# Two layers and a second block on one core: products over 64 rows of the array widened to all 128

## The chip, the cores and the metric

The kernel runs on one core of a Trainium2 chip. The metric is the device time of one execution in microseconds (us), and less is better. TensorE is called PE here (its weight loads PEld), VectorE DVE, ScalarE ACT, GpSimd POOL, SyncE SP.

## What is computed

512 tokens of 2048 features pass through two equal layers and then a second block. Each layer multiplies x by a wide matrix, feeds three branches (a short convolution, a causal attention with eight heads, a linear recurrence called rwkv), mixes them with a second matrix and normalises. The second block has a differential attention with eight heads and a state space branch. Three places matter here. In the rwkv branch of both layers:

```python
r, wd, k, v, ad = _split(xs, RWKV_SHIFT_SIZES)          # wd, ad: 64 features each
w = -jax.nn.softplus(-(w0 + jnp.tanh(wd) @ w2)) - 0.5   # w2: 64 x 512
a = jax.nn.sigmoid(a0 + ad @ a2)                        # a2: 64 x 512
```

In the attention of both layers the scores of a head are a product over 192 features, 128 of its own and 64 rotary ones whose key all heads share:

```python
q = jnp.concatenate([q_nope, _rope(q_pe, cos, sin)], axis=-1)
k = jnp.concatenate([k_nope, jnp.broadcast_to(k_pe, (B, S, MLA_HEADS, QK_ROPE))], axis=-1)
s = jnp.einsum('bqhd,bkhd->bhqk', qb, k, preferred_element_type=jnp.float32) * scale
```

In the second block each head has two score maps, each a product over 64 features:

```python
s = jnp.einsum('bqhcd,bkhcd->bhcqk', q_blk, k).astype(jnp.float32) * scale
p = jax.nn.softmax(s, axis=-1)
w = p[:, :, 0] - lam * p[:, :, 1]
```

## The kernel before

Everything lies with features on the 128 partitions and the 512 tokens in the free dimension. Nearly all the work of PE is the wide products of `inproj` (L184 to L186): a weight is split into a high and a low part (ACT casts the high one at L169, DVE subtracts for the low one at L170), x is split in the same way, and of the four products three are made, tile by tile of 128 features. A tile of 128 output columns takes 16 tiles of features times three products, each 128 rows by 512 tokens.

Products over 64 features are handled in a more compact way. One operand holds its high part on one half of the partitions and its low part on the other half, the second operand holds its high part on both halves, so that one product over 128 rows gives high times high and low times high. What is missing, high times low, is a second product over the 64 partitions of the own half. There are three such places:

- `rank_product` (L481): L484 over 128 rows, L485 over 64 rows, 512 tokens each. It is called twice by `rwkv_prep` for each of four pairs of heads, in two layers: 16 times. `rwkv_lora` (L463 to L478) makes its operands; one tile `wl` holds the low parts of both weights, on a half each.
- `scores` in `mla_branch` (L921): for each of four query tiles L929 over 128 rows, L930 over 64 rows, then L931 over 128 rows in plain float32; eight heads, two layers: 64 times.
- `diff_scores` (L1585): for each of four query tiles and two components L1632 over 128 rows, L1633 over 64 rows; eight heads: 64 times. Component 0 lies on partitions 0 to 63, component 1 on 64 to 127, and one tile `kl` holds the low parts of the keys of both.

The query tiles have 256, 256, 384 and 512 columns.

No order is written by hand. The framework orders the instructions of each engine from its own estimate of durations, and each engine then runs its list strictly in order. Tiles come from pools with a fixed number of slots; a tile whose slot is still in use waits. In the second block the attention's pool `qa` has 20 slots under the tag `a`, handed out in turn. Constants (masks, the rotary tables `cos` and `sin`) live in the pool `cp` for the whole kernel.

In each layer the masked products of a chunk (L560) give DVE and POOL the blocks to be inverted in `rwkv_inverse` (L598, L599); PE meanwhile works on other columns, and the first instruction of PE that needs the inverse's space is L664 in `rwkv_chunks`, which reads what was spilled to DRAM under the name `pack`. POOL's sums of squares (L774) and small powers (L397) of the low rank projections stand in POOL's list ahead of its share of the inverse.

Of the kernel before, what the change touches and what calls it, by code (L numbers as in the profile page):

```python
# [19 lines left out]
P = 128  # L20
S = 512
# [34 lines left out]
# column starts in w_in  # L56
# [3 lines left out]
# rows of the packed layer parameters  # L60
# [13 lines left out]
class K:  # L74
    """What every part of the kernel shares: engines, pools, constants."""
# [23 lines left out]
    def open(self, name, psum, side=None, **bufs):  # L99
        """pools for one part of the kernel: slots of 2 KB, and of 4 KB where the tag ends in 4; psum: its banks.  # L100
        To be closed; tags of the parts around it stay in use."""
# [43 lines left out]
    def load_w(self, parts, kt, n, side=False):  # L145
        """parts: [(source [kt*P, m], first column of the tile)]; for each k the two exact parts, or one tile of
        them side by side."""
# [26 lines left out]
    def split(self, src, hi, lo, eng=None):  # L174
        """hi + lo == src, each in eleven bits of mantissa."""
        self.nc.scalar.copy(hi, src)
        return (eng or self.nc.vector).tensor_tensor(out=lo, in0=src, in1=hi.bitcast(F32), op=ALU.subtract)  # L177

    def mm3(self, out, w, x, first=True, last=True):
        """out[m, n] (+)= sum over k of w[k][., m] x[k][., n] in three passes; w, x: lists of (hi, lo)."""  # L180
# [13 lines left out]
    def inproj_group(self, x, cols, pss):  # L194
        """several tiles of columns at once, tile by tile of x as they come"""
# [11 lines left out]
def bc_last(ap, n):  # L207
    """[p, a] seen as [p, a, n]"""
    return ap.unsqueeze(2).to_broadcast([ap.shape[0], ap.shape[1], n])


def consts(k: K):
# [5 lines left out]
    # blk[p, q] = 1 where p and q lie in the same block of 64, blk32 of 32  # L218
# [9 lines left out]
    # [s, (strict t > s, incl t >= s)] in each block of 64  # L228
    k.mrk = cp.tile([P, P], F32, name="mrk")
# [6 lines left out]
    # scan resets: zero at the start of each 64  # L236
    k.rst = cp.tile([P, S], F32, name="rst")
    nc.gpsimd.memset(k.rst, 1.0)
    nc.gpsimd.memset(k.rst.rearrange("p (c t) -> p c t", t=64)[:, :, 0:1], 0.0)
    # causal: 0 where key <= query, NEG elsewhere, [q, k]  # L240
# [4 lines left out]
    # dup[p, m]: the sum of the two halves of the rows, onto both  # L245
    k.dup = cp.tile([P, P], F32, name="dup")
# [9 lines left out]
def rope_tables(k: K, positions):  # L256
    nc, cp = k.nc, k.cp
    k.cos = cp.tile([P, S], F32, name="cos")
    k.sin = cp.tile([P, S], F32, name="sin")
# [21 lines left out]
    # with the sign of the product that goes to the other half of each 64  # L281
# [4 lines left out]
def _reduce_angle(self, ang):  # L286
    """ang less its nearest multiple of two pi"""
# [15 lines left out]
def layer_params(k: K, a, l):  # L303
    """The per-feature vectors of a layer, one column each; in two steps."""
# [45 lines left out]
    # 1 - mu, half of w0 and a0, 1 - k_a  # L350
# [10 lines left out]
def tok_sums(k: K, tiles, rhs, ncol, width=None):  # L361
    """[128 tokens, 4, ncol] of sum over features of tile * rhs column; tiles: list of [P, S]"""
# [8 lines left out]
def bcast_cols(k: K, cols, nh):  # L371
    """PSUM [P, S] whose row p, column t is cols[t % 128, t // 128, head of p]; cols: SBUF [P, 4, nh]"""
# [13 lines left out]
def rsqrt_cols(k: K, ps, shape, scale, eps, floor=None):  # L386
    """(scale * ps + eps) ** -0.5, or max(ps, floor) ** -0.5"""
# [13 lines left out]
def gate2(k: K, ps, out=False):  # L401
    """2 * silu of a PSUM tile; out: let go of the tile soon"""
# [11 lines left out]
def shifted(k: K, ps, mu, omu, tag=None):  # L414
    """token shift of a projection: (1 - mu) u + mu * (u one token earlier)"""
# [33 lines left out]
def rwkv_first(k: K, x, w):  # L449
    """the products for the ranks of the decay and the rate and for the first pair of heads"""  # L450
# [7 lines left out]
def rwkv_lora(k: K, a, l, ps, col, der):  # L458
# [4 lines left out]
    # for products in two passes: of the decay's and the rate's ranks the high part on their own half of the partitions  # L463
    # and the low one on the other, the weights' high part on both and the low one on the own
    hs, out, wl = (slice(0, 64), slice(64, 128)), [], k.b(dt=F32R)
    for q, key in enumerate(("rwkv_w2", "rwkv_a2")):
# [5 lines left out]
        wh, r = k.b(dt=F32R), k.b(dt=F32R)  # L472
        nc.scalar.copy(wh, w2)
        nc.vector.tensor_tensor(out=wl[own], in0=w2[own], in1=wh.bitcast(F32)[own], op=ALU.subtract)
        nc.scalar.copy(r[own], wa[own])
        nc.vector.tensor_tensor(out=r[other], in0=wa[own], in1=r.bitcast(F32)[own], op=ALU.subtract)
        out.append((wh, r, wl, own))
# [3 lines left out]
def rank_product(k: K, ranks, c):  # L481
    (wh, r, wl, own), cols = ranks, slice(c, c + P)
    ps = k.ps()
    k.nc.tensor.matmul(ps, lhsT=wh[:, cols], rhs=r, start=True, stop=False)  # L484
    k.nc.tensor.matmul(ps, lhsT=wl[own, cols], rhs=r[own], start=False, stop=True)  # L485
# [3 lines left out]
# a pair of heads' operands for 128 tokens, in floats of a row: [B|K] of the first chunk of 64 and [K|B] of the  # L489
# second; V, its chunks swapped; A; R; for each head and chunk the masked products [B|K] x [A|R], [s, (A|R, t)]  # L490
# [12 lines left out]
def rwkv_prep(k: K, l, j, rkv, col, der, ranks, pe, T, pack, sbg):  # L503
# [3 lines left out]
    # decay: log w = -(c/2)(1 + tanh(z/2)), its sums over each chunk  # L507
# [13 lines left out]
    # in-context rate  # L521
# [4 lines left out]
    # kk = normalised k * k_k  # L526
# [6 lines left out]
    # A = -kk * Pex ; B = kk * a / P ; K = k' / P ; R = r * P  # L533
# [20 lines left out]
    # products of the tokens of a chunk  # L554
# [16 lines left out]
    # bonus: (sum over a head of r k' r_k) v  # L571
# [7 lines left out]
def rwkv_inverse(k: K, T, TI):  # L579
    """inverses of the 64 x 64 blocks on the diagonal of 1 - T, row by row of T; of each block one partition has  # L580
    the even rows and another the odd ones"""
# [12 lines left out]
    def step(eng, X, tmp, q, n, w):  # L594
        """the first n rows of X, whose last w columns come after T's row q"""
# [30 lines left out]
def rwkv_chunks(k: K, pe, pack, TI, Y):  # L626
    """the states and outputs of all heads, 128 tokens of two pairs at a time"""
# [938 lines left out]
def ssm_glu(k: K, a, yp, src, sz):  # L1566
# [15 lines left out]
    return out  # L1582


def diff_scores(k: K, hd, x, w, first):  # L1585
    nc = k.nc
    V, G = nc.vector, nc.gpsimd
    hm = k.hm
# [211 lines left out]
```

## Time and profile before

| | |
|---|---|
| three runs | 3482.21, 3482.34, 3485.09 us; median 3482.34 us |
| profiled execution, first to last instruction | 3480.9 us |
| PE busy | 97% of the span, 15603 matmul records |
| DVE, ACT, POOL busy | 58%, 34%, 25% |
| mean granted clock of PE | 0.980 of full speed |
| HBM traffic | 364.93 MB read, 92.27 MB written |

A matmul's busy time in this profile is longer than its share of the engine, because matmuls overlap: L184 has a mean of 398 ns although one starts every 0.23 us. So what a matmul costs is read from the distance of starts in the timeline, not from its duration. The time of the profiled execution itself is not listed apart from the three runs; its span is 1.4 us below their median.

### The profile page before, as it was taken

The page shows a single profiled execution, that of the slowest core. Times are in us where ns is not written, and L with a number is a line of the kernel's source. Part 1 is how long each engine was busy: PE and PEld are TensorE (multiplying, and loading weights), DVE is VectorE, ACT ScalarE, POOL GpSimd, SP SyncE. Part 2 cuts the span into 40 slices and gives each one's busy share as a digit, 9 for nine tenths or more (in the row PEclk, how much of TensorE's full clock was granted, in tenths as well). Part 3 has the DMA queues.
Part 4 walks back from the last instruction along what each step waited for, and adds up shares of the span by engine and source line. Part 5 has one row for each costly group of instructions (what it writes and reads, how often), then busy time and mean ns, then how long its engine had stood idle before and what let it go on. Part 6 is the DMA issues. An engine that isn't in the chain of part 4 may idle for free.

```text
span 3480.9 us, 41882 instructions
## 1 busy us (share of the span) xinstructions
PE 3360.1 (97%) x15603; PEld 2666.2 (77%) x15603; DVE 2003.3 (58%) x3035; ACT 1194.4 (34%) x1950; POOL 861.0 (25%) x974
## 2 busy tenths in 40 slices
PE   8999899999999998999988999999999999999999
PEld 7777688777867776887767666777777888888887
DVE  4546645655754466355589688878787532332332
ACT  4332223543533322224457233333333422222332
POOL 1224322003411143230035233333333000000011
PEclk9999999999989999999999899999999999999999
DMA  6455445335644454443256343433433733333443
GB/s 174 146 171 151 128 126 154 104 101 146 209 135 134 148 148 134 121 153 116 76 183 221 99 131 106 121 112 116 119 115 94 228 106 108 105 100 106 151 141 117
DMA packets 687934, 466.27 MB, mean 134 GB/s; under 512 B 91285, under 2 KB 621994, under 8 KB 687730
## 3 DMA queue, kind: packets, MB, share of 16 engines
q1 hardware_dynamic: 687730, 463.59, 44.9%
q8 instruction: 123, 2.02, 0.3%
q14 instruction: 81, 0.66, 0.1%
HBM read 364.93 MB, written 92.27 MB: 131 GB/s over the span
## 4 chain that ended last, share of the span: by engine, by line
PE 40%; DVE 9%; issue 3%; DMA 1%; ACT 1%; POOL 0%; SPq 0%; DVEq 0%; ACTq 0%
PE acc L186 10%; PE acc L185 10%; PE acc L184 10%; PE ps_b L186 2%; PE ps_b L185 2%; PE ps_b L184 2%; DVE wl L170 1%; DVE s L1537 1%; DVE x L1541 1%; PE ps_s L1552 1%; PE ps_s L931 1%; PE ps_a L1633 1%; DVE x L1542 1%; DVE b L1159 1%; DVE x L1538 1%
## 5 line engine op out<-in xcount | busy, mean ns | idle before, releaser
L186 PE MATMUL acc<-xh,wl 128*128 128x512 f32 x3552 | 1409.9, 397 | 19.4 <-DVE wl L170 19.4
L184 PE MATMUL acc<-xh,wh 128*128 128x512 f32 x3552 | 1406.7, 398 | 10.3 <-ACT u L1501 4.9
L185 PE MATMUL acc<-xl,wh 128*128 128x512 f32 x3552 | 1410.5, 397 | 2.2 <-DVE xl L177 2.2
L170 DVE TENSOR_TENSOR wl<-wr,wh 128x1024 fp32r<-128x1024 f32 (+1 forms) x508 | 676.3, 1332 | 820.1 <-ACT wh L169 807.4
L169 ACT CAST wh<-wr 128x1024 fp32r<-128x1024 f32 (+1 forms) x508 | 530.5, 1044 | 1529.7 <-PE acc L185 1208.4
L186 PEld LDWEIGHTS acc<-xh,wl 128*128 128x128 f32 x3552 | 674.6, 190 | 175.3 <-DVE wl L170 24.6
L184 PEld LDWEIGHTS acc<-xh,wh 128*128 128x128 f32 x3552 | 674.8, 190 | 167.5 <-issue 12.4
L185 PEld LDWEIGHTS acc<-xl,wh 128*128 128x128 f32 x3552 | 674.3, 190 | 164.3 <-issue 20.2
L1733 POOL TENSOR_TENSOR b<-b,b 128x512 f32<-128x512 f32 x16 | 20.9, 1309 | 496.1 <-DVE b L1731 496.1
L1532 POOL TENSOR_TENSOR s<-s,s 128x512 f32<-128x512 f32 x32 | 44.7, 1397 | 263.0 <-DVE s L1531 256.0
L1731 DVE SCALAR_TENSOR_TENSOR b<-b,ps_b 128x512 f32<-128x512 f32 x32 | 22.0, 688 | 106.0 <-PE ps_b L186 106.0
L1154 POOL TENSOR_TENSOR b<-b,b 128x512 f32<-128x512 f32 x28 | 46.7, 1667 | 112.1 <-DVE b L1137 97.4
L397 POOL TENSOR_TENSOR rr_a<-rv_a,mhalf 128x8 f32<-128x8 f32 (+1 forms) x24 | 46.6, 1940 | 108.8 <-DVE rv_a L392 108.8
L1552 PE MATMUL ps_s<-x,s 128*32 128x512 f32 x128 | 46.9, 672 | 27.4 <-DVE x L1541 27.4
L1540 POOL TENSOR_TENSOR s<-s,x 128x512 f32<-128x512 f32 x32 | 52.0, 1625 | 82.9 <-DVE x L1538 58.5
L1474 POOL TENSOR_TENSOR r<-r,r 128x512 f32<-128x512 f32 x32 | 55.8, 1744 | 63.3 <-DVE r L1473 57.5
L961 POOL TENSOR_TENSOR v<-v,c 128x512 f32<-128x512 f32 x16 | 20.6, 1286 | 204.6 <-ACT v L958 197.2
L598 DVE TENSOR_TENSOR pk<-pk,pk 128x224 f32<-128x224 f32 (+59 forms) x126 | 65.4, 519 | 4.5 <-DMA pk<-T 1.1
L599 DVE TENSOR_TENSOR pk<-pk,pk 128x224 f32<-128x224 f32 (+59 forms) x126 | 64.4, 511 | 3.5
L655 POOL COPY zm_pk<-pk 64x128 f32<-64x128 f32 x64 | 27.1, 424 | 151.3 <-DMA pk<-pack 138.0
L819 ACT ACTIVATE a<-ps_a,nm_a,sp_a 128x128 f32<-128x128 f32 (+3 forms) x64 | 39.2, 615 | 69.9 <-DVE nm_a L816 65.8
L563 DVE TENSOR_TENSOR pk<-ps_m,mrk 128x512 f32<-128x512 f32 x32 | 22.1, 691 | 68.3 <-PE ps_m L560 68.2
(497 smaller groups left out, 4486.0 us busy)
## 6 DMA issues: line engine op xcount, KB each, us to landing
wr<-in_w_in_dram SPq DMA_DIRECT2D x336, 512.0 KB
wr<-in_w_out_dram SPq DMA_DIRECT2D x96, 512.0 KB
pack<-pk SPq DMA_DIRECT2D x32, 576.0 KB
pk<-pack SPq DMA_DIRECT2D x32, 576.0 KB
CS<-r SPq DMA_DIRECT2D x32, 512.0 KB
s<-CS SPq DMA_DIRECT2D x32, 512.0 KB
b<-xd SPq DMA_DIRECT2D x48, 256.0 KB
c<-mix SPq DMA_DIRECT2D x32, 256.0 KB
```

The lines of the kernel that those rows point to most:

```text
L169: nc.scalar.copy(hi[:, : m * n], raw[:, : m * n])
L170: nc.vector.tensor_tensor(out=lo[:, : m * n], in0=raw[:, : m * n], in1=hi.bitcast(F32)[:, : m * n], op=ALU.subtract)
L184: self.nc.tensor.matmul(out, lhsT=wh, rhs=xh, start=st, stop=False)
L185: self.nc.tensor.matmul(out, lhsT=wh, rhs=xl, start=False, stop=False)
L186: self.nc.tensor.matmul(out, lhsT=wl, rhs=xh, start=False, stop=sp)
L397: nc.gpsimd.tensor_tensor(out=r.rearrange(flat), in0=v.rearrange(flat), in1=k.mhalf[:, 0:n], op=ALU.pow)
L598: eng.tensor_tensor(out=t3, in0=X[:, 0:n, c - 1 : c].to_broadcast([P, n, w]), in1=q[:, q.shape[1] - w :].unsqueeze(1).to_broadcast([P, n, ...
L599: eng.tensor_tensor(out=X[:, 0:n, c:], in0=X[:, 0:n, c:], in1=t3, op=A)
L1154: nc.gpsimd.tensor_tensor(out=sums[0], in0=sums[0], in1=t, op=ALU.add)
L1474: nc.gpsimd.tensor_tensor(out=x, in0=x, in1=m, op=SB)
L1540: G.tensor_tensor(out=t1, in0=sn, in1=t2, op=M)
L1552: nc.tensor.matmul(py[o], lhsT=lc[:, d, o], rhs=xs[p][d], start=(d == 0), stop=(d == 1))
```

## The change

The second product runs over all 128 rows in all three places. For the rank products each weight gets a low part on both halves (`wl` inside the loop, and six slots in the pool `wa` in place of five). For the attention of the layers the shared key's low part was already on both halves, so only the slices go. In the second block each component gets a low tile of its own, whose other half is zero; `diff_lows` makes two such pairs once and sets the zeros with four POOL instructions, and heads use the pairs in turn. With two halves multiplied, the rank products and the layers' scores now also contain low times low; in the second block the zeros leave the result as it was. Five constants of the two layers move to a pool `lp` that closes ahead of the second block, and `qa` has 19 slots under `a` in place of 20.

```diff
 def rwkv_lora(k: K, a, l, ps, col, der):
...
-    hs, out, wl = (slice(0, 64), slice(64, 128)), [], k.b(dt=F32R)
+    hs, out = (slice(0, 64), slice(64, 128)), []
...
-        wh, r = k.b(dt=F32R), k.b(dt=F32R)
+        wh, r, wl = k.b(dt=F32R), k.b(dt=F32R), k.b(dt=F32R)
         nc.scalar.copy(wh, w2)
-        nc.vector.tensor_tensor(out=wl[own], in0=w2[own], in1=wh.bitcast(F32)[own], op=ALU.subtract)
+        nc.vector.tensor_tensor(out=wl, in0=w2, in1=wh.bitcast(F32), op=ALU.subtract)
...
 def rank_product(k: K, ranks, c):
...
-    k.nc.tensor.matmul(ps, lhsT=wl[own, cols], rhs=r[own], start=False, stop=True)
+    k.nc.tensor.matmul(ps, lhsT=wl[:, cols], rhs=r, start=False, stop=True)
...
     def scores(hd, pair):
...
-            nc.tensor.matmul(ps[:, 0:m], lhsT=qp[h][hs, ts], rhs=kpl[hs, 0:m], start=False, stop=False)
+            nc.tensor.matmul(ps[:, 0:m], lhsT=qp[h][:, ts], rhs=kpl[:, 0:m], start=False, stop=False)
...
-        with k.phase(f"p{l}a", {"x": 3, "m": 1}, w=10, r=5, pk=2, wa=5):
+        with k.phase(f"p{l}a", {"x": 3, "m": 1}, w=10, r=5, pk=2, wa=6):
...
+def diff_lows(k: K):
+    out = []
+    for _ in range(2):
+        kl = [k.small((P, S), f"kl{c}", 2, F32R) for c in range(2)]
+        for c, t in enumerate(kl):
+            k.nc.gpsimd.memset(t[64 - 64 * c : 128 - 64 * c].bitcast(F32), 0.0)
+        out.append(kl)
+    return out
...
-def diff_scores(k: K, hd, x, w, first):
+def diff_scores(k: K, hd, x, w, first, kl):
...
-        qs, ks, kl = [k.b(dt=F32R) for _ in range(2)], [k.b(dt=F32R) for _ in range(2)], k.b(dt=F32R)
+        qs, ks = [k.b(dt=F32R) for _ in range(2)], [k.b(dt=F32R) for _ in range(2)]
...
-            V.tensor_tensor(out=kl[own], in0=kr[own], in1=ks[c].bitcast(F32)[own], op=ALU.subtract)
+            V.tensor_tensor(out=kl[c][own], in0=kr[own], in1=ks[c].bitcast(F32)[own], op=ALU.subtract)
...
-                nc.tensor.matmul(ps[:, 0:m], lhsT=qs[c][halves[c], i * P : n], rhs=kl[halves[c], 0:m], start=False, stop=True)
+                nc.tensor.matmul(ps[:, 0:m], lhsT=qs[c][:, i * P : n], rhs=kl[c][:, 0:m], start=False, stop=True)
...
-    att = k.open("qa", {"a": 3}, "right", a=20)
+    att = k.open("qa", {"a": 3}, "right", a=19)
...
+        with k.use("a", "a"):
+            lows = diff_lows(k)
...
-                nxt = diff_scores(k, q, x, w, first[1:] if q == 0 else [])
+                nxt = diff_scores(k, q, x, w, first[1:] if q == 0 else [], lows[q % 2])
...
 def fused_kernel(ctx: ExitStack, tc: tile.TileContext, a, out, dbg=None):
     k = K(ctx, tc, dbg)
+    layers = ExitStack()
+    k.lp = layers.enter_context(tc.tile_pool(name="lp", bufs=1))
...
         x, xd = first_layer(k, a, l, x, xd, *k.par[l])
+    layers.close()
     second_block(k, a, x, xd, out)
```

The tiles `mrk`, `rst`, `dup`, `cos` and `sin` take `k.lp` where they took `cp`.

The number of instructions stays the same on PE, DVE, ACT and SP; POOL has four more. The framework's order moves in places. Three are shown, in the names that the program gives its tiles; the line numbers of the changed kernel differ, since L1632 and L1633 became L1642 and L1643.

The first is PE in the second block, at the first head's scores (`ps_a` is the score tile, `acc` a wide product in progress). Before:

```order
L1632 MATMUL ps_a_16856<-a_16773,a_16771 128x256
L1633 MATMUL ps_a_16856<-a_16775,a_16771 128x256
L186 MATMUL acc_17068<-xh_16339,wl_17064 128x512
L184 MATMUL acc_17068<-xh_16348,wh_17063 128x512
L1632 MATMUL ps_a_16869<-a_16774,a_16772 128x256
L185 MATMUL acc_17068<-xl_16349,wh_17063 128x512
L1633 MATMUL ps_a_16869<-a_16775,a_16772 128x256
L186 MATMUL acc_17068<-xh_16348,wl_17064 128x512
```

With the change:

```order
L1642 MATMUL ps_a_16869<-a_16787,a_16785 128x256
L1643 MATMUL ps_a_16869<-kl_a_16412,a_16785 128x256
L186 MATMUL acc_17081<-xh_16344,wl_17077 128x512
L184 MATMUL acc_17081<-xh_16353,wh_17076 128x512
L1642 MATMUL ps_a_16882<-a_16788,a_16786 128x256
L185 MATMUL acc_17081<-xl_16354,wh_17076 128x512
L1643 MATMUL ps_a_16882<-kl_a_16413,a_16786 128x256
L186 MATMUL acc_17081<-xh_16353,wl_17077 128x512
```

Nothing moved here: the second product of a score tile has products over 128 rows on both sides in either list, and reads `kl_a` in the new one.

The second is PE in the first layer around L664, the first use of what the inverse leaves free. Before:

```order
L186 MATMUL acc_3928<-xh_139,wl_3918 128x512
L184 MATMUL acc_3928<-xh_150,wh_3917 128x512
L664 MATMUL ps_t_2749<-ident,pk_2740 128x128 x4
L185 MATMUL acc_3928<-xl_151,wh_3917 128x512
L186 MATMUL acc_3928<-xh_150,wl_3918 128x512
```

With the change:

```order
L185 MATMUL acc_3864<-xl_164,wh_3853 128x512
L186 MATMUL acc_3864<-xh_164,wl_3854 128x512
L184 MATMUL acc_3864<-xh_175,wh_3853 128x512
L664 MATMUL ps_t_2753<-ident,pk_2744 128x128 x4
L185 MATMUL acc_3864<-xl_176,wh_3853 128x512
```

L664 now stands one column tile earlier (`acc_3864` is the tile that was `acc_3860`, the one ahead of `acc_3928`): 42 wide products that preceded it now follow it, and 43 in the second layer. The last masked products L560 stand 32 wide products earlier too in the first layer, and 41 in the second.

The third is POOL in the first layer, ahead of its share of the inverse (`la` and `c`: sums of squares, `pk` and `t_pk`: the inverse). Before:

```order
L635 MEMSET zq_pk_2731 128x512
L397 TENSOR_TENSOR rr_c_2495<-rv_c_2493,mhalf 128x4
L608 MEMSET pk_2010 128x1024
L608 MEMSET pk_2011 128x512
L610 MEMSET pk_2010 64x16 x2
L610 MEMSET pk_2011 64x16 x2
L774 TENSOR_TENSOR la_2506<-la_2506,c_2636 128x512
L397 TENSOR_TENSOR rr_c_2648<-rv_c_2646,mhalf 128x4
L598 TENSOR_TENSOR t_pk_2012<-pk_2011,pk_2086 128x31
```

With the change:

```order
L774 TENSOR_TENSOR la_2221<-la_2221,c_2351 128x512
L608 MEMSET pk_2014 128x1024
L608 MEMSET pk_2015 128x512
L774 TENSOR_TENSOR la_2221<-la_2221,c_2419 128x512
L610 MEMSET pk_2014 64x16 x2
L610 MEMSET pk_2015 64x16 x2
L774 TENSOR_TENSOR la_2221<-la_2221,c_2487 128x512
L397 TENSOR_TENSOR rr_c_2499<-rv_c_2497,mhalf 128x4
L774 TENSOR_TENSOR la_2510<-la_2510,c_2640 128x512
L598 TENSOR_TENSOR t_pk_2016<-pk_2015,pk_2090 128x31
```

Three of the sums moved from ahead of the clearing instructions to among them, and the last L397 moved behind the first steps of the inverse.

## Rows read from the trace of the kernel before

**Rows 1.** The page: span, and part 1 for PE (busy us, share, instructions).
```profile
span 3480.9 us, 41882 instructions
...
PE 3360.1 (97%) x15603; PEld 2666.2 (77%) x15603; DVE 2003.3 (58%) x3035; ACT 1194.4 (34%) x1950; POOL 861.0 (25%) x974
```
**Rows 2.** Timeline of PE, rank products: start, us, line, out<-in, rows*columns, moving operand.
```profile
74.41 0.39 PE L484 MATMUL ps_x<-wa,wa 128*128 128x512 f32 x1
74.73 0.50 PE L485 MATMUL ps_x<-wa,wa 64*128 64x512 f32 x1
75.16 0.49 PE L484 MATMUL ps_x<-wa,wa 128*128 128x512 f32 x1
75.58 0.49 PE L485 MATMUL ps_x<-wa,wa 64*128 64x512 f32 x1
76.01 0.50 PE L184 MATMUL acc<-xh,wh 128*128 128x512 f32 x1
76.35 0.40 PE L185 MATMUL acc<-xl,wh 128*128 128x512 f32 x1
76.59 0.40 PE L186 MATMUL acc<-xh,wl 128*128 128x512 f32 x1
```
**Rows 3.** Timeline of PE in the second block: products over 96 rows.
```profile
2010.01 0.63 PE L1528 MATMUL ps_s<-us_s,s 96*128 96x512 f32 x2
2010.48 0.39 PE L186 MATMUL acc<-xh,wl 128*128 128x512 f32 x1
```
**Rows 4.** Timeline of PE's weight loads at the rank products.
```profile
74.19 0.19 PEld L484 LDWEIGHTS ps_x<-wa,wa 128*128 128x128 f32 x1
74.73 0.18 PEld L485 LDWEIGHTS ps_x<-wa,wa 64*128 64x128 f32 x1 [0.35 <-issue]
```
**Rows 5.** Stages of layer one: us; busy (count) PE, PEld, DVE, ACT, POOL; clock.
```profile
60.00:285.00 225.00, 223.41 (x1054) 176.28 (x1053) 102.03 (x121) 71.33 (x96) 62.51 (x96) 1.00 0.53 161
...
600.00:790.00 190.00, 188.81 (x851) 140.78 (x849) 111.63 (x246) 92.33 (x198) 19.14 (x20) 1.00 0.40 120
```
**Rows 6.** The same for one head of the second block, in two parts.
```profile
2304.00:2347.00 43.00, 43.00 (x182) 32.27 (x183) 25.67 (x61) 20.33 (x37) 2.38 (x3) 1.00 0.39 114
2347.00:2396.00 49.00, 45.13 (x205) 32.38 (x205) 48.36 (x56) 10.53 (x23) 31.30 (x19) 0.97 0.39 115
```
**Rows 7.** Timeline of PE in the second block: one score tile of 256 columns.
```profile
2140.50 0.28 PE L1632 MATMUL ps_a<-a,a 128*128 128x256 f32 x1
2140.71 0.38 PE L1633 MATMUL ps_a<-a,a 64*128 64x256 f32 x1
2141.02 0.50 PE L184 MATMUL acc<-xh,wh 128*128 128x512 f32 x1
2141.35 0.39 PE L185 MATMUL acc<-xl,wh 128*128 128x512 f32 x1
```
**Rows 8.** Timeline of PE in the layers' attention: products of 256 columns over 128 rows.
```profile
658.51 0.28 PE L915 MATMUL acc<-wh,n 128*128 128x256 f32 x1
...
658.86 0.28 PE L915 MATMUL acc<-wh,n 128*128 128x256 f32 x1
```
**Rows 9.** Timeline of PE in the layers' attention: a score tile.
```profile
641.15 0.28 PE L929 MATMUL ps_s<-n,q 128*128 128x256 f32 x1
641.36 0.38 PE L930 MATMUL ps_s<-n,q 64*128 64x256 f32 x1
641.67 0.49 PE L931 MATMUL ps_s<-q,q 128*128 128x128 f32 x2
```
**Rows 10.** Waits of PE, second block (1990 to 2700): total us, times, longest.
```profile
PE ps_s L1552 <- DVE x L1541: 27.4, 12, 4.0
```
**Rows 11.** Waits of PE during the first layer's inverse (285 to 376).
```profile
PE ps_t L664 <- DMA pk<-pack: 15.3, 1, 15.3
```
**Rows 12.** Timeline of POOL: its first step of that inverse.
```profile
318.55 1.30 POOL L598 TENSOR_TENSOR t_pk<-pk,pk 128x31 f32<-128x31 f32 x1 [2.91 <-DMA pk<-T]
```
**Rows 13.** Line L635: a POOL clearing instruction, ns min/median/max.
```profile
L635 POOL MEMSET zwh_pk<- x4: 518/523/529, 283.1 to 1250.7; 128x512 f32 x4
```

More of the change, by code (lines that the diff above doesn't have):

```diff
@@ L227, in consts @@
     k.hm = k.blk64.rearrange("p (h w) -> p h w", w=64)[:, :, 0]
-    k.mrk = cp.tile([P, P], F32, name="mrk")
+    k.mrk = k.lp.tile([P, P], F32, name="mrk")
     mk = k.b((P, 2, P))
@@ L235, in consts @@
         nc.gpsimd.tensor_copy(out=k.mrk[a : a + 64].rearrange("p (i t) -> p i t", i=2), in_=mk[a : a + 64, :, a : a + 64])
-    k.rst = cp.tile([P, S], F32, name="rst")
+    k.rst = k.lp.tile([P, S], F32, name="rst")
     nc.gpsimd.memset(k.rst, 1.0)
@@ L244, in consts @@
                             channel_multiplier=1)
-    k.dup = cp.tile([P, P], F32, name="dup")
+    k.dup = k.lp.tile([P, P], F32, name="dup")
     for half in (0, 64):
@@ L257, in rope_tables @@
     nc, cp = k.nc, k.cp
-    k.cos = cp.tile([P, S], F32, name="cos")
-    k.sin = cp.tile([P, S], F32, name="sin")
+    k.cos = k.lp.tile([P, S], F32, name="cos")
+    k.sin = k.lp.tile([P, S], F32, name="sin")
     row = k.b()
@@ L471, in rwkv_lora @@
             nc.sync.dma_start(out=w2[h], in_=a[key][l])
-        wh, r = k.b(dt=F32R), k.b(dt=F32R)
+        wh, r, wl = k.b(dt=F32R), k.b(dt=F32R), k.b(dt=F32R)
         nc.scalar.copy(wh, w2)
-        nc.vector.tensor_tensor(out=wl[own], in0=w2[own], in1=wh.bitcast(F32)[own], op=ALU.subtract)
+        nc.vector.tensor_tensor(out=wl, in0=w2, in1=wh.bitcast(F32), op=ALU.subtract)
         nc.scalar.copy(r[own], wa[own])
         nc.vector.tensor_tensor(out=r[other], in0=wa[own], in1=r.bitcast(F32)[own], op=ALU.subtract)
-        out.append((wh, r, wl, own))
+        out.append((wh, r, wl))
     return out
 def rank_product(k: K, ranks, c):
-    (wh, r, wl, own), cols = ranks, slice(c, c + P)
+    (wh, r, wl), cols = ranks, slice(c, c + P)
     ps = k.ps()
     k.nc.tensor.matmul(ps, lhsT=wh[:, cols], rhs=r, start=True, stop=False)
-    k.nc.tensor.matmul(ps, lhsT=wl[own, cols], rhs=r[own], start=False, stop=True)
+    k.nc.tensor.matmul(ps, lhsT=wl[:, cols], rhs=r, start=False, stop=True)
     return ps
@@ L923, in scores @@
         h = hd % 2
-        hs = slice(h * 64, h * 64 + 64)
         prs = []
```

## Prediction

> **What bounds the kernel now.** I read the page first: PE is busy for 97% of a span of 3480.9 us, DVE for 58% [rows 1]. Matmuls overlap in this profile, so 97% only says that PE is rarely without work, not that it works at its best pace. The next view is therefore the timeline of PE, where the distance between starts tells what each matmul really takes.
>
> At the rank products the reader sees the price of a change of width [rows 2]. Between two neighbours over 128 rows with 512 columns the distance is 0.24 us (76.35 to 76.59). From a product over 128 rows to one over 64 it is 0.32 (74.41 to 74.73), from the 64 rows back to 128 it is 0.43 and 0.43 (74.73 to 75.16, 75.58 to 76.01), and the neighbour after that is late too: 0.34 (76.01 to 76.35). A product over 96 rows pays nothing of this: two of them and the step to L186 take 0.47, which is 0.235 each [rows 3]. So it isn't a matter of rows left idle; something is paid at the border between 64 rows and more, in both directions. The weight loads show the same border: the load of L484 starts at 74.19, a whole matmul ahead of its product at 74.41, while that of L485 starts at 74.73, together with its own product [rows 2, 4].
>
> Then the stages. In the part of a layer with the rank products PE is busy for 223.41 of 225 us and DVE for 102.03; in the one with the attention scores PE has 188.81 of 190 and DVE 111.63 [rows 5]. The second layer repeats both. A head of the second block has two faces: while its scores are made PE is busy all 43 us and DVE 25.67, and in the state space part DVE is the full one with 48.36 of 49 us, PE having 45.13 [rows 6].
>
> **The change, part by part.**
>
> *Rank products, 16.* From L484 at 74.41 to L185 at 76.35 there are five steps in 1.94 us [rows 2]. At 0.235 each they would be 1.18. The two products over 64 rows therefore cost 0.76 together, 0.38 each. Widened, they have neighbours of the same kind on both sides and take the common pace. 16 x 0.38 = 6.1 us, all of it on the path, since PE is what fills that stage [rows 5].
>
> *Scores of the second block, 64.* From L1632 at 2140.50 to L185 at 2141.35 are 0.85 us for two products of 256 columns and one of 512 [rows 7]. The pace of 256 columns over 128 rows is a third of 658.51 to 658.86, 0.117 [rows 8]. Expected without a border: 2 x 0.117 + 0.235 = 0.47. The excess is again 0.38. 64 x 0.38 = 24.3 us. The wider tiles cross the same borders, so I use one number for all.
>
> *Scores of the layers' attention, 64.* The steps into and out of L930 are 0.21 and 0.31 [rows 9], equal to those of L1633 (2140.50 to 2140.71, 2140.71 to 2141.02) [rows 7], so the same 0.38 applies: 24.3 us, in a stage that PE fills [rows 5].
>
> Together 54.7 us of PE's time. The ends for the unknown price of the widened product: it cannot well save more, for that a step would have to be below the common pace, and no row shows one; it may save less, if only the two steps around the product go and the lateness of the one after them stays. Without that last step, which is 0.10 too long (2141.02 to 2141.35, less 0.235) [rows 7], it is 0.28 each, or 40 us. I take 0.38, since 96 rows pass with no lateness on either side [rows 3].
>
> *How much of it arrives.* The first 30.4 us lie in stages that PE fills, and I count them whole. In the second block the scores lie in the 43 us where PE is full and DVE is not [rows 6], so the 8 products of a head bring the state space part forward by 3 us. That part is DVE's, and PE waits in it for L1541, 27.4 us in 12 waits over all heads [rows 10]. It is as long as before and only starts earlier, but some of it overlaps the neighbour's scores. I take off a tenth, 2.4 us; all of it (24.3) is the rival below.
>
> *The order.* Widening changes the framework's estimates and with them its lists. At the inverse of the first layer PE has 42 wide products fewer ahead of L664, where it already waits 15.3 us [rows 11], but the last L560, which starts the inverse, also comes 32 products earlier. The difference is 10 x 0.235 = 2.4 us more wait, and 2 x 0.235 = 0.5 in the second layer. That holds if the inverse really starts earlier: POOL's share begins when its transfer of T has landed, POOL itself having been free for 2.91 us [rows 12]. The sums that moved closer to it stand in a list that has this much to spare. I count 2.9 us lost; the ends are 10 gained (two thirds of the wait of one layer [rows 11]) and 20 lost (below). Scattered moves elsewhere pass between products of equal pace, and I count them as nothing, covered by PE's full list; if they open gaps, they widen the range.
>
> *DVE, ACT, SP.* The four subtractions for `wl` cover twice the partitions with the same 512 elements on each. DVE is idle for 123 of the 225 us there [rows 5], so even doubled they would lie beside PE's work. The low parts of the keys are written by the same 16 instructions. No transfer is added; SP's list has the same transfers.
>
> *POOL.* Four clearing instructions are added ahead of the second block. The nearest row is a clearing of 128 x 512 with 0.52 us [rows 13]: 2.1 us at most, on an engine with a quarter of its time in use [rows 1]. Behind them stands the power for the first head's query norm, whose input comes only after the first products of the block. I count nothing, at most 2.1.
>
> *Slots.* `qa` loses one slot, and one tile per head, the low part of the keys, no longer takes a slot in turn. The turn has one tile less and one slot less; for tiles whose life doesn't span that turn it is one slot tighter. The longest wait that I read for a single tile in the block is 4.0 us [rows 10]; once a head that would be 32 us, but nothing in the list of waits points at it. I count nothing. The pool `lp` issues no instruction.
>
> **The sum.** 6.1 + 24.3 + 24.3 - 2.4 - 2.9 = 49.4 us. The profiled execution has a span of 3480.9 us [rows 1]; around it lie 1.4 us up to the median of the three runs, 3482.34, which I keep. 3482.3 - 49.4 = 3433 us. A measurement of this kernel can tell about 0.2%, 7 us, from no change.
>
> **The rivals.**
>
> *The second block swallows its share.* DVE is the full engine for 49 of a head's 92 us [rows 6]. If its list, not PE's, sets the pace over the whole head, what PE gains at the scores comes back as longer waits at L1552. For it speaks [rows 10]; against it, that DVE is idle for 17 of the 43 us in the scores' part. Then 30.4 - 2.9 = 27.5 us remain: 3455 us.
>
> *The inverse does not come earlier.* If POOL's share of the inverse is held by the sums that now stand right ahead of it, PE reaches L664 sooner and waits longer: (42 + 43) x 0.235 = 20 us in place of 2.9, so 3450 us. Against it speaks the 2.91 us to spare [rows 12] and that DVE's share starts from L560 alone.
>
> *The border isn't about rows.* If the excess came from the operand (the same stationary tile loaded twice, a second product into a fresh score tile), widening would leave it. The rank products argue against it, because there both operands differ and the price is equal. Then only the order counts: 3485 us, no change.
>
> *Loads lose their cover, the other side.* The second product's load would be slower to start if a load can run ahead only into rows that the running matmul does not use. Half the rows are free for L485 when only the other half is busy; none would be after the change. Each of the 144 products would then stand for its own load, 0.19 us [rows 4], on top of today's time: 144 x 0.19 = 27 us, with 2.9 for the order 3513 us. It decides from the point where the load of the widened product starts with its product and not a matmul earlier. Against it stands L484: its load over all 128 rows starts at 74.19, while the matmul before it, L186, is still to be finished [rows 4]. The Trainium skill has this rule (TensorE: Matmul & The Clock Gate, "The mechanism" under packing small matmuls): loads overlap with matmuls in flight only when their row groups differ. By that rule the change would lose; the trace does not agree, since here it is the load over half the rows that is late, by 0.35 us of idle loader, and the loads over all rows that run ahead.
>
> **How the numbers follow.** The forecast has 0.68, the second block as the bound 0.13, the inverse that stays 0.09, no effect 0.05, loads uncovered 0.05. The likeliest gives 3433 us. Its own bounds are 54.7 and a gain of 10 at the inverse, 3418, and 40 less 5.3, 3448. The range takes in the two rivals on the same side, to 3457, and at the low end 2 us more for scattered moves, 3416. Faster by over 0.2%: 0.90 (the first three). Within 0.2%: 0.05. Slower: 0.05.
>
> **What would show it.** In the timeline the three second products appear with 128 rows, the steps around them are 0.23 (512 columns) and 0.12 (256 columns), and their loads start a matmul earlier. The stages with rank products and scores of a layer are shorter by 3 and 12 us each, the first part of a head in the second block by 3, and DVE's part keeps its length. PE's wait at L664 is 15 to 20 us. The forecast is wrong if the steps stay at 0.3 and more, if waits at L1552 grow from 27.4 towards 50 us, or if the wait at L664 passes 25 us.

## The result, and the profile after

The changed kernel takes 3427.07 us (median of 4 runs, 3423.93 to 3428.52), the kernel before 3482.28 on the same chip: 55.2 us less, a ratio of 0.984 with a 95% interval of 0.983 to 0.985. The prediction was 3433 with a range of 3416 to 3457.

The page of the profiled execution (3426.18 us), to be read against [rows 1]:

```profile
span 3424.4 us, 41918 instructions
...
PE 3306.3 (97%) x15603; PEld 2666.6 (78%) x15603; DVE 1995.6 (58%) x3035; ACT 1191.6 (35%) x1950; POOL 860.8 (25%) x978
```

PE has the same 15603 matmul records and is busy for 53.8 us less, while its weight loads are busy for the same time. PE's share of 97% did not move: it said nothing about what could be gained.

The timeline of PE at the rank products, where [rows 2] stood, and the weight loads beside [rows 4]:

```profile
74.33 0.39 PE L484 MATMUL ps_x<-wa,wa 128*128 128x512 f32 x1
74.55 0.39 PE L485 MATMUL ps_x<-wa,wa 128*128 128x512 f32 x1
74.78 0.39 PE L484 MATMUL ps_x<-wa,wa 128*128 128x512 f32 x1
75.01 0.39 PE L485 MATMUL ps_x<-wa,wa 128*128 128x512 f32 x1
75.23 0.39 PE L184 MATMUL acc<-xh,wh 128*128 128x512 f32 x1
75.46 0.39 PE L185 MATMUL acc<-xl,wh 128*128 128x512 f32 x1
```
```profile
74.33 0.19 PEld L485 LDWEIGHTS ps_x<-wa,wa 128*128 128x128 f32 x1
```

The five steps from L484 to L185 take 1.13 us in place of 1.94; the steps of 0.32 and 0.43 and the late neighbour behind are all gone. L485's load starts at 74.33, together with the product ahead of its own, which starts at 74.55. A score tile of the second block, beside [rows 7], took 0.85 us from L1632 to the second wide product behind; now it takes 0.47:

```profile
2103.87 0.28 PE L1642 MATMUL ps_a<-a,a 128*128 128x256 f32 x1
2103.99 0.28 PE L1643 MATMUL ps_a<-kl_a,a 128*128 128x256 f32 x1
2104.11 0.40 PE L184 MATMUL acc<-xh,wh 128*128 128x512 f32 x1
2104.34 0.39 PE L185 MATMUL acc<-xl,wh 128*128 128x512 f32 x1
```

What a whole stage saved stands in the rows that group a line's instructions, with the first and the last start. Before, the rank products of layer one, the scores of layer one and those of the second block:

```profile
L485 PE MATMUL ps_x<-wa,wa x8: 491/494/498, 74.7 to 229.8; 64*128 64x512 f32 x8
...
L930 PE MATMUL ps_s<-n,q x32: 379/408/498, 641.4 to 764.7; 64*128 64x256 f32 x16, 64*128 64x384 f32 x8, 64*128 64x512 f32 x8
...
L1633 PE MATMUL ps_a<-a,a x64: 379/434/579, 2057.4 to 2701.7; 64*128 64x256 f32 x32, 64*128 64x384 f32 x16, 64*128 64x512 f32 x16
```

After:

```profile
L485 PE MATMUL ps_x<-wa,wa x8: 389/389/389, 74.6 to 226.7; 128*128 128x512 f32 x8
...
L929 PE MATMUL ps_s<-n,q x32: 278/310/393, 642.9 to 754.2; 128*128 128x256 f32 x16, 128*128 128x384 f32 x8, 128*128 128x512 f32 x8
...
L1643 PE MATMUL ps_a<-kl_a,a x64: 278/337/416, 2024.0 to 2644.0; 128*128 128x256 f32 x32, 128*128 128x384 f32 x16, 128*128 128x512 f32 x16
```

From the first to the last start, 155.1 us became 152.1 (3.0 less), 123.3 became 111.3 (12.0 less) and 644.3 became 620.0 (24.3 less). In the latter two, 31 and 63 of the second products lie between the first start and the last, so each saves 0.39 us. In layer two the rank products save 3.0 us as well (1041.6 to 1195.6 before, 1030.2 to 1181.2 after).

One head of the second block in its two parts, beside [rows 6] (us; busy of PE, PEld, DVE, ACT, POOL; clock):

```profile
2262.00:2302.00 40.00, 40.00 (x184) 32.26 (x183) 25.75 (x62) 20.62 (x38) 2.10 (x2) 1.00 0.41 120
2302.00:2351.00 49.00, 45.12 (x205) 32.06 (x203) 48.55 (x56) 10.12 (x22) 31.30 (x19) 0.97 0.39 116
```

The part with the scores went from 43 to 40 us, the part that DVE fills stayed at 49. PE's longest wait in the second block and around the inverse of layer one, after, beside [rows 10, 11]:

```profile
PE ps_s L1551 <- DVE x L1540: 27.2, 11, 3.9
...
PE ps_t L664 <- DMA pk<-pack: 13.7, 1, 13.7
```

Around the inverse of layer two, before and then after:

```profile
PE ps_t L664 <- DMA pk<-pack: 16.2, 1, 16.2
...
PE ps_t L664 <- DMA pk<-pack: 4.1, 1, 4.1
PE ps_s L377 <- POOL rr_c L397: 3.1, 1, 3.1
```

The second block waits as before. The wait at L664 fell from 15.3 to 13.7 us in layer one and from 16.2 to 4.1 in layer two; part of it stands as smaller waits at other places.

What the new order is worth can be read from the first L485 of a layer to its first score product, a stretch with the inverse in it and with the same number of matmul records in either kernel. Layer one is in the rows above: 566.7 us (74.7 to 641.4) became 568.3 (74.6 to 642.9), although its rank products save 3.0, so 4.6 us were lost there. In layer two, before and then after:

```profile
L485 PE MATMUL ps_x<-wa,wa x8: 491/500/502, 1041.6 to 1195.6; 64*128 64x512 f32 x8
L930 PE MATMUL ps_s<-n,q x32: 379/408/498, 1606.5 to 1729.9; 64*128 64x256 f32 x16, 64*128 64x384 f32 x8, 64*128 64x512 f32 x8
...
L485 PE MATMUL ps_x<-wa,wa x8: 389/389/394, 1030.2 to 1181.2; 128*128 128x512 f32 x8
L929 PE MATMUL ps_s<-n,q x32: 278/310/393, 1587.5 to 1698.9; 128*128 128x256 f32 x16, 128*128 128x384 f32 x8, 128*128 128x512 f32 x8
```

There 564.9 us became 557.3, 7.6 less where the rank products give 3.0: 4.6 us were gained. The two layers cancel.

### The profile page after: what moved, and what is told of

Read it like the earlier page. It is cut to its first block, busy times and chain, and to the rows that moved or that the text cites. A ratio compares the mean times of both kernels' runs of the same rounds, so it can differ in the third digit from the quotient of the medians.

```text
span 3424.4 us, 41918 instructions
## 1 busy us (share of the span) xinstructions
PE 3306.3 (97%) x15603; PEld 2666.6 (78%) x15603; DVE 1995.6 (58%) x3035; ACT 1191.6 (35%) x1950; POOL 860.8 (25%) x978
## 4 chain that ended last, share of the span: by engine, by line
PE 38%; DVE 10%; issue 3%; DMA 1%; ACT 1%; POOL 1%; SPq 0%; DVEq 0%; POOLq 0%; ACTq 0%
PE acc L185 10%; PE acc L186 10%; PE acc L184 10%; PE ps_b L186 2%; PE ps_b L185 2%; PE ps_b L184 2%; DVE wl L170 2%; DVE s L1536 1%; DVE x L1540 1%; DVE x L1541 1%; PE ps_s L1551 1%; DVE x L1537 1%; DVE b L1158 1%; DVE x L1538 1%; PE ps_s L930 1%
## 5 line engine op out<-in xcount | busy, mean ns | idle before, releaser
L184 PE MATMUL acc<-xh,wh 128*128 128x512 f32 x3552 | 1404.6, 397 | 17.4 <-ACT c L772 5.0
L185 PE MATMUL acc<-xl,wh 128*128 128x512 f32 x3552 | 1410.3, 397 | 1.9 <-DVE xl L177 1.9
L184 PEld LDWEIGHTS acc<-xh,wh 128*128 128x128 f32 x3552 | 675.6, 190 | 171.1 <-issue 12.6
L185 PEld LDWEIGHTS acc<-xl,wh 128*128 128x128 f32 x3552 | 675.8, 190 | 161.8 <-issue 18.0
L1551 PE MATMUL ps_s<-x,s 128*32 128x512 f32 x128 | 47.0, 681 | 27.3 <-DVE x L1540 27.2
L397 POOL TENSOR_TENSOR rr_a<-rv_a,mhalf 128x8 f32<-128x8 f32 (+1 forms) x24 | 46.5, 1939 | 103.2 <-DVE rv_a L392 103.2
L1763 POOL TENSOR_TENSOR b<-b,ln 128x512 f32<-128x512 f32 x16 | 20.7, 1292 | 152.2 <-DVE b L1762 125.7
```

Source lines behind the costliest of these rows:

```text
L184: self.nc.tensor.matmul(out, lhsT=wh, rhs=xh, start=st, stop=False)
L185: self.nc.tensor.matmul(out, lhsT=wh, rhs=xl, start=False, stop=False)
L397: nc.gpsimd.tensor_tensor(out=r.rearrange(flat), in0=v.rearrange(flat), in1=k.mhalf[:, 0:n], op=ALU.pow)
L1551: nc.tensor.matmul(py[o], lhsT=lc[:, d, o], rhs=xs[p][d], start=(d == 0), stop=(d == 1))
```

## Experiments

The theory: PE pays some 0.39 us where it goes from a product over all rows to one over 64 and back, a border in what follows; all of it lies on the path. Diffs are against the changed kernel. Each time is the median of four runs (`masked128` has five, `u_all` ten). Kernels of one group shared a chip; times of different groups are compared by their ratio to the kernel before, with its 95% interval in brackets.

**The three edits undone one by one, and all together** (`u_rank`, `u_layer`, `u_second`, `u_all`). Only the slices go back; tiles, pools and zeros stay.

```diff
-    k.nc.tensor.matmul(ps, lhsT=wl[:, cols], rhs=r, start=False, stop=True)
+    k.nc.tensor.matmul(ps, lhsT=wl[own, cols], rhs=r[own], start=False, stop=True)
```
```diff
-            nc.tensor.matmul(ps[:, 0:m], lhsT=qp[h][:, ts], rhs=kpl[:, 0:m], start=False, stop=False)
+            nc.tensor.matmul(ps[:, 0:m], lhsT=qp[h][hs, ts], rhs=kpl[hs, 0:m], start=False, stop=False)
```
```diff
-                nc.tensor.matmul(ps[:, 0:m], lhsT=qs[c][:, i * P : n], rhs=kl[c][:, 0:m], start=False, stop=True)
+                nc.tensor.matmul(ps[:, 0:m], lhsT=qs[c][halves[c], i * P : n], rhs=kl[c][halves[c], 0:m], start=False, stop=True)
```

> The changed kernel with only the 16 rank products (the second one of each) back on the 64 rows of their own half; tiles, pools and everything else stay. Border theory: 16 x 0.38 to 0.40 us come back, so 6.1 to 6.4 us over the changed kernel's 3427, all of it in the two stages with the rank products; give or take 5 for the order at the inverse. Rival 'the order did it': the undone products cost nothing, 3427. Rival 'loads lose their cover': it would be faster than 3427.

> The changed kernel with only the 64 scores of the layers' attention (the product with the shared key's low part) back on 64 rows. Border theory: 64 x 0.38 to 0.40, so 24 to 26 us over 3427, 12 to 13 in each layer: 3451 to 3453. Rival 'the order did it': under 5 us. Rival 'the price is at the operand and not at the rows': under 5 us too, but then the timeline still shows steps of 0.12 around this product.

> The changed kernel with only the 64 score products of the second block back on 64 rows; the low tiles of the keys, their zeros and the 19 slots stay. Border theory with full arrival: 64 x 0.38 to 0.40, so 24 to 26 us over 3427, about 3 per head. Rival 'the second block swallows its share': 0 to 5 us, with the waits of PE for the state space part shorter by as much. My forecast took off a tenth: 22.

> The changed kernel with all 144 second products back on 64 rows, and all else of the change kept: the low tile per weight, six slots, the key's low tiles with zeros, 19 slots, the pool that closes after the layers. If the three prices add up and the rest of the change is worth nothing: the sum of the three single undos, 55 to 57 us over 3427, which is the time of the kernel before, 3482. If tiles, slots and pools bring some of the gain, it stays below 3482 by that; if they cost, it lies above.

Measured beside 3481.61 us of the kernel before: 3431.58, 3451.66, 3453.22 and 3481.73 us in this order, with ratios of 0.9857 (0.9837 to 0.9877), 0.9913 (0.9898 to 0.9928), 0.9917 (0.9902 to 0.9932) and 1.000 (0.999 to 1.0009). Against 3427.07 these are 4.5, 24.6, 26.2 and 54.7; the three single ones add up to 55.3. The smallest can't be told from the changed kernel's time by its interval, but its 3.0 us per layer stand in the traces above. All of the gain is in the widths; tiles, pools, zeros and order are worth nothing together. The order did change the waits: with all products narrow PE waits 12.9 and 4.7 us at L664, much as in the changed kernel. From the first L485 to the first score product `u_all` takes 570.0 us in layer one (74.5 to 644.5), 3.3 more than the kernel before, and 561.1 in layer two (1044.5 to 1605.6), 3.8 less. At the first product over 96 rows the trace stands at 2010.04 us where the kernel before has 2010.01 [rows 3].

**A price for each product, or for each border** (`pair_same`)

```diff
-                nc.tensor.matmul(ps[:, 0:m], lhsT=qs[c][:, i * P : n], rhs=kl[c][:, 0:m], start=False, stop=True)
+                nc.tensor.matmul(ps[:, 0:m], lhsT=qs[c][halves[c], i * P : n], rhs=kl[c][halves[c], 0:m], start=False, stop=False)
+                nc.tensor.matmul(ps[:, 0:m], lhsT=qs[c][halves[c], i * P : n], rhs=kl[1 - c][halves[c], 0:m], start=False, stop=True)
```

> As the run with only the second block's scores on 64 rows (3453 us), and behind each of these 64 products another one over the same 64 rows, whose low tile holds zeros there. All 64 stand right next to each other in PE's list. Border theory (the price is paid at the change between 64 rows and more, once for a group): only the columns of the added products, 0.12 + 0.12 + 0.17 + 0.17 + 0.23 + 0.23 and another 0.12 + 0.12 for the two tiles of 256, 1.28 us a head, 10 in all: 3463. Theory 'each product over 64 rows has its own price': 64 x 0.4 more on top, 3489.

Measured 3464.24 us, ratio 0.9961 (0.9946 to 0.9976): 11 over the median of `u_second`, 15 by the ratios, 10.1 by the spans of the profiles (3461.0 and 3450.9). That fits the columns of the added products alone, 10; the 26 us more of a price for each product are outside. Timeline of a pair:

```profile
2101.49 0.40 PE L185 MATMUL acc<-xl,wh 128*128 128x512 f32 x1
2101.82 0.38 PE L1643 MATMUL ps_a<-kl_a,a 64*128 64x256 f32 x1
2102.04 0.28 PE L1644 MATMUL ps_a<-kl_a,a 64*128 64x256 f32 x1
2102.25 0.50 PE L186 MATMUL acc<-xh,wl 128*128 128x512 f32 x1
2102.59 0.40 PE L184 MATMUL acc<-xh,wh 128*128 128x512 f32 x1
```

From L185 to L184 it is 1.10 us for two wide products (0.46) and two of 256 columns (0.24): an excess of 0.40, as for a single one. So the price is paid for the border and not for each product. (A pair on opposite halves into the same score tile was not tried.)

**Fewer idle rows, more idle rows** (`rows96`, `rows32`)

```diff
-                nc.tensor.matmul(ps[:, 0:m], lhsT=qs[c][:, i * P : n], rhs=kl[c][:, 0:m], start=False, stop=True)
+                e = slice(0, P if c else 96)
+                nc.tensor.matmul(ps[:, 0:m], lhsT=qs[c][e, i * P : n], rhs=kl[c][e, 0:m], start=False, stop=True)
```
```diff
+                e = slice(64 * c, 64 * c + 32)
```

> The changed kernel with the second product of the second block's component 0 over 96 rows (64 that count and 32 zeros), component 1 over 128. If the price is for rows that are left idle, 32 products of 96 rows cost a part of 0.38 each, some 6 to 12 us: 3433 to 3439. If it is paid only where the number of rows falls to 64: 3427.

> The changed kernel with the second product of the second block's scores over 32 rows (half of the low term is left out). If fewer rows cost more, it lies clearly above the 3453 us of the run with 64 rows there, toward 3480. If the price is that of the change alone, it is as with 64 rows, 3453; a price between is possible, since no product over 32 rows stands between wide ones in the traces so far.

Measured 3422.11 us, ratio 0.984 (0.9825 to 0.9854), equal to the changed kernel's, and 3447.30, ratio 0.9907 (0.9892 to 0.9922), where 64 rows had 0.9917. Timelines, 96 rows and then 32:

```profile
2097.56 0.28 PE L1642 MATMUL ps_a<-a,a 128*128 128x256 f32 x1
2097.67 0.28 PE L1644 MATMUL ps_a<-kl_a,a 96*128 96x256 f32 x1
2097.79 0.39 PE L184 MATMUL acc<-xh,wh 128*128 128x512 f32 x1
```
```profile
2098.61 0.28 PE L1642 MATMUL ps_a<-a,a 128*128 128x256 f32 x1
2098.82 0.38 PE L1644 MATMUL ps_a<-kl_a,a 32*128 32x256 f32 x1
2099.13 0.50 PE L184 MATMUL acc<-xh,wh 128*128 128x512 f32 x1
2099.47 0.39 PE L185 MATMUL acc<-xl,wh 128*128 128x512 f32 x1
```

The products over 96 rows step like those over 128 (0.11 and 0.12 us), those over 32 like those over 64 (0.21, 0.31, 0.34). Idle rows cost nothing in themselves. The Trainium skill (TensorEngine Tiling (Array Packing), "Key Properties") says that a change of tiling mode drains TensorE. The traces agree with a price on the change and show how much it is, 0.39 to 0.40 us there and back; that it is a drain, none of them shows.

**How much of PE's time in the second block arrives** (`wide_twice`)

```diff
-                nc.tensor.matmul(ps[:, 0:m], lhsT=qs[c][:, i * P : n], rhs=kl[c][:, 0:m], start=False, stop=True)
+                nc.tensor.matmul(ps[:, 0:m], lhsT=qs[c][:, i * P : n], rhs=kl[c][:, 0:m], start=False, stop=False)
+                nc.tensor.matmul(ps[:, 0:m], lhsT=qs[c][:, i * P : n], rhs=kl[c][:, 0:m], start=False, stop=True)
```

> The changed kernel with the widened second product of the second block's scores made twice (the output then has the low term twice). It measures what a plain product over all rows costs there and how much of PE's time in this stage arrives at the end: 1.28 us a head by the pace of 0.117, 0.173 and 0.230 us, 10.2 in all: 3437 if all of it arrives. Rival 'DVE sets the pace of the second block': 3427 to 3430.

Measured 3441.25 us, ratio 0.9891 (0.9874 to 0.9907): 14 to 17 us over the changed kernel, more than the 10.2 of the products themselves. DVE as the pace of the block is refuted. The surplus goes with the granted clock of PE: over 2050 to 2700 us its mean is 0.95 (0.97 in the changed kernel), and between 2000 and 2720 us it stands at 0.50 for 68.0 us in all (37.4 in the changed kernel). Of the four runs the one with a mean clock of 0.981, like the changed kernel's, took 3437.58 us, which is what was expected; those with 0.980, 0.977 and 0.976 took 3440.36, 3442.15 and 3445.34. One place in this run, PE having waited 3.0 us at L1551 just before (2158.03 to 2161.03):

```profile
2162.00:2170.00 8.00, 8.00 (x22) 5.87 (x21) 7.83 (x12) 1.57 (x2) 7.57 (x4) 0.50 0.36 111
```

and the same place of the changed kernel, behind two shorter waits (2.9 us together):

```profile
2172.00:2180.00 8.00, 8.00 (x35) 5.77 (x35) 7.52 (x9) 5.26 (x9) 4.72 (x3) 1.00 0.58 180
```

The clock is the last figure but two: 0.50 is 1.2 GHz, and PE makes 22 matmuls in 8 us in place of 35. Why the clock fell more often in this run was not tested.

**The rule carried on to what still has borders** (`after_again`, `masked128`, `affine128`, `both128`). The masked products of a pair of heads, with both heads' operand in one tile that is zero where they mix:

```diff
-            for h in range(2):
-                hs = slice(h * 64, h * 64 + 64)
-                nc.tensor.matmul(ps[:, h, c * P : c * P + P], lhsT=pk[hs, i, O_BK + c * P : O_BK + c * P + P],
...
+            nc.tensor.matmul(ps[:, c, 0:256], lhsT=pk[:, i, O_BK + c * P : O_BK + c * P + P],
+                             rhs=k.az[:, i].rearrange("p g (c t) -> p g c t", c=2)[:, :, c], start=True, stop=True)
```

and the products over 6 rows at the end of a layer:

```diff
-        nc.tensor.matmul(pr, lhsT=gb[o, q % 4], rhs=r6[o], start=True, stop=True)
+        nc.tensor.matmul(pr, lhsT=gb[:, q], rhs=r6, start=True, stop=True)
```

> The changed kernel itself, unaltered, beside the three that follow, so that they can be compared with it on one chip: 3422 to 3429 us.

> The border theory carried to another place. The masked products of a chunk (L560) are four products over 64 rows and 128 columns in a group of their own; 32 groups stand between wide products. From the wide product before to the second wide one behind, a group takes 1.302 us in the trace of the changed kernel, 0.846 more than the two wide ones at 0.228. Here one product over 128 rows and 256 columns makes both heads of a chunk, with zeros where the heads mix; plain float32 with 256 columns steps by 0.22 at L930, so a group is 0.44: 32 x 0.40 = 13 us less, 3414, if nothing else becomes late. Two more copies on ACT per pair of heads lie ahead of the first product; if they or the zeros hold the start of the inverse, up to 5 of it are lost. Rival 'the price was special to second products into a started tile': no gain, 3427.

> The same for the 32 products over 6 rows at the end of a layer (L1242), in 14 groups between wide ones: the scale and shift rows get a tile of their own for each tile of features, zero elsewhere, and the product takes all 128 rows. Eight of the groups cost 0.40 to 0.45 us over the pace, 3.3 in all; six stand where PE waits for DVE's work of the tiles anyway, so that 0 to 4 of theirs arrives. 3420 to 3424, near to what a measurement can tell.

> Both of the last two edits in the changed kernel. The stages are apart, so the gains should add: 3427 - 13 - 4 = 3410, between 3406 and 3418. If this holds, it beats the kernel before and the changed one.

Measured 3425.31 (3422.07 to 3427.36), 3425.32 (3421.81 to 3427.09), 3417.43 (3415.40 to 3419.03) and 3415.99 us (3415.47 to 3421.31), with ratios of 0.9842, 0.9843, 0.982 (0.9807 to 0.9834) and 0.982 (0.9806 to 0.9833). Two of the four expectations missed, those of `masked128` (3414) and `affine128` (3420 to 3424). That of `both128` (3406 to 3418) was met by luck: of the two gains that it adds up, one did not come and the other came out larger.

The masked products gained nothing. Timeline of a group in the changed kernel, and then widened:

```profile
166.13 0.39 PE L185 MATMUL acc<-xl,wh 128*128 128x512 f32 x1
166.45 0.72 PE L560 MATMUL ps_m<-pk 64*128 64x128 f32 x8
167.10 0.50 PE L186 MATMUL acc<-xh,wl 128*128 128x512 f32 x1
167.44 0.39 PE L184 MATMUL acc<-xh,wh 128*128 128x512 f32 x1
```
```profile
165.24 0.39 PE L185 MATMUL acc<-xl,wh 128*128 128x512 f32 x1
165.47 1.02 PE L561 MATMUL ps_m<-az_w,pk 128*128 128x256 f32 x4
166.14 0.58 PE L186 MATMUL acc<-xh,wl 128*128 128x512 f32 x1
166.56 0.40 PE L184 MATMUL acc<-xh,wh 128*128 128x512 f32 x1
```

From L185 to L184 it is 1.31 and 1.32 us. The border did go: the step into the group is 0.23 us in place of 0.32. But the widened products take twice what I had set. A plain float32 product has two records here, and 0.22 us is the step of one: two products have four records, 0.86 us in place of 0.44. In the narrow form the products of the two heads lie on opposite halves and run side by side (single records start 6 to 7 ns apart), so that the doubled columns eat the saved border.

The 6-row products gained 7.9 us between the medians. In the changed kernel and with 128 rows:

```profile
976.06 0.39 PE L1242 MATMUL ps_r<-b,b 6*128 6x512 f32 x1
976.38 0.50 PE L185 MATMUL acc<-xl,wh 128*128 128x512 f32 x1
976.72 0.39 PE L186 MATMUL acc<-xh,wl 128*128 128x512 f32 x1
```
```profile
976.16 0.39 PE L1245 MATMUL ps_b<-b,gz_b 128*128 128x512 f32 x1
976.38 0.39 PE L185 MATMUL acc<-xl,wh 128*128 128x512 f32 x1
976.61 0.39 PE L186 MATMUL acc<-xh,wl 128*128 128x512 f32 x1
```

Of the eight groups at full clock seven lost the whole excess of 0.40 to 0.45 us and one keeps 0.12. That is 1.6 us at the end of the first layer, but from the first to the last of these products it takes 21.3 us there in place of 26.1 (`after_again`), 4.8 less. Most of the rest goes with the clock. Over the 45 us from 945 on, in the changed kernel and with 128 rows:

```profile
945.00:990.00 45.00, 40.02 (x149) 27.99 (x148) 32.30 (x55) 15.28 (x23) 14.56 (x11) 0.77 0.50 157
...
945.00:990.00 45.00, 39.08 (x165) 30.06 (x165) 34.24 (x57) 17.68 (x26) 16.64 (x12) 0.85 0.57 178
```

The mean clock went from 0.77 to 0.85, and 45 x 0.08 = 3.6 us, an estimate. Which of the two came first was not tested, but the traces of the other runs bear on it. The twelve traces with the 6-row products, those of the kernels before and after among them, have 24 ends of a layer: the clock stood at 0.50 around these products for 20.5 us in 19 of them, for 17.1 in three and for 13.6 or 13.7 in two. In the four ends with 128 rows it was 10.2, 13.7, 17.1 and 20.5 us. So the clock also came back early without the edit, though seldom. From the first to the last of these products all four took less (20.4 to 22.5 us) than any of the 24 (23.4 to 26.2). `both128` adds nothing to `affine128`. Both beat the changed kernel: the ranges of their runs and of `after_again`'s don't overlap.

## Why the prediction was right, and where its sum failed

*The price, "0.38 each": right.* It is 0.39 by the stages and 0.40 by single places, there and back, and the lateness of the next product, on which the lower end of 40 us hung, went as taken. 144 x 0.39 = 56 us, against 55.2 measured. The reason drawn from the 96-row products [rows 3] held when 96 rows were put in the place in question (`rows96`).

*Rank products 6.1, layers' scores 24.3: right.* The first showed 3.0 us per layer in the trace, the second 24.6 when undone.

*"I take off a tenth, 2.4 us": this step failed.* All 24.3 us of the second block arrived, 26.2 when undone. The two parts of a head stand behind one another and don't overlap in a way that costs: DVE is idle for 14 of the 40 us of the scores, so its part starts as much earlier as PE is done sooner, and the waits at L1551 stayed at 27.2 us (27.4 before, [rows 10]).

*"I count 2.9 us lost" for the order: right in layer one, this step failed in layer two.* It has 2.4 us lost in the first layer; `u_all`, with the changed kernel's order and narrow products, lost 3.3 there and the changed kernel 4.6. It has 0.5 lost in the second; there `u_all` gained 3.8 and the changed kernel 4.6. That the order comes out at nothing on the whole is luck, since the two layers cancel; the kernel before has one trace to compare with. The sign that it set, a wait of 15 to 20 us at L664, was missed in both layers. In layer one the waits around the inverse are 13.7 + 3.8 + 0.8 = 18.3 us, near the 17.7 that the step gave, but they stand at three places. In layer two they are 9.7 in place of 16.2; from the last L560 to L664 it takes 84 us there, 90 before. Which transfer or engine made that shorter was not followed. These two deductions, 2.4 and 2.9 us, are nearly all of the 6 us between 3433 and 3427.

*Costs set at nothing: right.* The four clearing instructions took 0.52 us each on POOL around 1963 us, and nothing waits for them; slots and pools show no price in `u_all`.

*The rivals.* That the second block swallows its share fell with `u_second` and `wide_twice`; that the inverse stays, with the wait of 13.7 us at L664; that the border isn't about rows, with `rows96` and the single undos. That loads lose their cover fell with the load row above: between products over all rows they start a matmul ahead, and PEld is busy for the same time. The prediction's reading, that loads over all rows run ahead and those over half are late, holds only there: in the kernel before, the second L484's load, behind a product over 64 rows, starts at 75.16, together with its own product [rows 2]. The Trainium skill's rule on row groups (TensorE: Matmul & The Clock Gate, "The mechanism" under packing small matmuls), that a load overlaps with matmuls in flight only where the row groups differ, does not hold between products over all 128 rows here. The same section also lets a load into a background weight buffer run ahead; whether that is what happens, no run here shows.

## What to carry to other kernels

Price a narrow product by the time from the wide product before to the second one behind, less the common pace: a lone product over 64, 32 or 6 rows between wide ones costs 0.40 us beyond its columns here, so zeros or unneeded rows up to 96 or 128 are cheaper. Leave groups alone whose products run side by side on opposite halves, and count the records of a product before using a step as its price. An edit that moves work past a wait is not worth the wait's change: in layer one the wait at L664 fell by 1.6 us and the stretch around it lost 4.6, in layer two it fell by 12.1 and the stretch gained 4.6. Look where the next stage starts.

## What was not expected of the hardware

The border costs the same for 64, 32 and 6 rows (0.40, 0.40, and 0.40 to 0.45 us), and once for a group. A pause of PE can cost more than itself: behind a wait of 3.0 us its clock was at 1.2 GHz for 8 us, though it was busy all that time. And at the end of a layer, where PE's clock was at 0.50 for 20.5 us in most traces, the kernels without borders got through these products in less time than the borders alone explain (4.8 us less at one end, of which the borders at full clock are 1.6); how much of that is the clock coming back sooner by chance is open.
